# Two transformer blocks on one core: returned expert rows by plain transfers, residual split and identity products later in each engine's order

## The chip, the cores and the metric

The kernel runs on one core of a Trainium2 chip. The metric is the device time of one execution in microseconds (us). A change is judged by the median of several executions of each kernel.

## The reference

Two blocks follow each other, each over 512 tokens of width 1024. Both end with the same kind of step, a mixture of experts (MoE) with two of 32 experts for each token, whose result is added to the residual `h`:

```python
tok_sorted = token_id[order]                 # first block; each token stands twice
hdn = lax.ragged_dot(xt[tok_sorted], w_e_in, group_sizes)
gate_h, up_h = jnp.split(hdn, 2, axis=-1)
ys = lax.ragged_dot(jax.nn.silu(gate_h) * up_h, w_e_out, group_sizes)
ys = ys * gates.reshape(-1)[order][:, None]
y = jnp.zeros_like(xt).at[tok_sorted].add(ys)
...
h = h + y
```

After the first MoE the sum is normalised twice (`rms_norm(h, norm_f_g)`, then the second block's `rmsnorm(h, g_mix)`) and multiplied by `w_in_2`. After the second MoE the sum is normalised with `g_final` and is the output.

## The kernel before, in words

The residual stays in SBUF as `K.h` (`hres` in the trace): four tiles `t` of 128 tokens x 1024. `moe` (from L923) is called twice. It works through 16 pairs of experts `p`; each expert has 64 places for tokens. For a pair, `first_products` (L1467, `gg`) multiplies the gathered tokens by the first weights, `glu` makes `sg` (ACT, then DVE at L1215), `turned` transposes it (`ap`, then `aT`), and `second_products` (L1480, `py`) multiplies by the second weights. The experts' weights stream through a ring of 1 MiB tiles (`rg`), issued on SP's queue in a fixed order (L920).

For pairs 0 to 13 `send` scales the rows and scatters them into a DRAM buffer `yd` by an indirect DMA of POOL's queue (L1264): each token has a row in the first half of `yd` (slot k = 0) and one in the second half (k = 1). After the last scatter `come_back` (L1267) brings `yd` back with eight transfers of 512 KiB on POOL's queue. In the second MoE all eight are accumulating DMAs into `K.h` (L1278). In the first MoE the four of k = 0 are accumulating and the four of k = 1 are plain loads into tiles `yb` (L1276), which take the place of the inputs' tiles `xnh`; `add_back` (L1283) adds them on DVE.

The rows of pairs 14 and 15 never go to DRAM. `gated` (L1240) splits the scaled rows into a high part (ACT, L1252) and a low part (DVE, L1253), both `y`, and makes a 0/1 matrix `C` (DVE, L1246 and L1247) that says which token each row belongs to. The first MoE multiplies `C` by `y` into PSUM (`combine`, L1293) and adds that to `K.h` (L1296).

The second MoE ends the kernel. There class `Sums` builds the final sum in PSUM (`f`): tile 0 of `K.h` by products with the identity in fp32 (`whole`, L1308), tiles 1 to 3 by `split` into a rounded high part (ACT, L1312) and a low part (DVE, L1313), which `halves` multiplies by a rounded identity (L1320). `add` (L1325) puts `C` times `y` on top. Tile 3 gets pair 14 by L1549 and L1551 first. `finish` then squares, normalises and writes the output. There `py_14` and `py_15` are late: their weights are the last of the stream, those of pair 15 in pieces.

What stands around the first MoE's end: `dense2` transposes `K.h` (`n2p`, L1726) into `ah` (ACT, L1727) and `al` (DVE, L1728), loads the first tiles `wr` of `w_in_2` (SP, L124), splits them into `wh` (ACT, L135) and `wl` (DVE, L138) and starts its products (`acc`, L146 to L148). POOL loads the gain row `gf` (L1720) and multiplies it with `K.h` into `fq` (L1739); ACT sums the squares of `fq` (`fk`, L230).

Each engine works its own list in order. The list is made when the program is built, by a scheduler that places an instruction as its inputs are expected; `after(K, x, y)` holds x behind y in the list and adds no wait on the chip. Tiles that lie in the same SBUF space wait for each other by semaphores.

## Time and profile before

| what | value |
|---|---|
| three runs | 1801.83, 1801.61, 1795.31 us; median 1801.61 |
| the profiled execution | 1793.93 us, its span 1792.2 us |
| PE busy | 1667.5 us (93%) |
| DVE, ACT, POOL busy | 796.2, 523.1, 297.7 us |
| DMA | 403.72 MB, mean 225 GB/s |
| end of the first MoE, first tiles of the second block | about 850 to 905 us |
| last stretch of the kernel, from the last scatter | 1701.6 to 1792.2 us |

Times in the trace count from the span's start. "Idle before <-X" in a timeline is idle time of that engine that X ended. A DMA's time runs from its issue to its landing. PEclk is the granted TensorE clock as a share of full speed: 1.00 is 2.4 GHz and 0.50 is 1.2 GHz.

### The profile page before, as it was taken

Reading aid. Unit: us, or ns where it says so; the run is one execution under the profiler, and the core shown is the slowest. Engines: PE = TensorE matmul, PEld = TensorE weight load, DVE = VectorE, ACT = ScalarE, POOL = GpSimd, SP = SyncE. Lnnn points to the kernel's source line nnn. Section 1 sums busy time; section 2 is a strip of 40 time slices with the busy share of each in tenths; the row PEclk is TensorE's granted clock in tenths of the full one; section 3 lists DMA queues with packets and bytes.
Section 4 is the critical chain, followed back from the end, with each engine's and each line's share of the span. In section 5 each row is a group of like instructions: output and inputs, shape, how many; then the busy total and the mean of one; then the engine's idle time right before and its main releaser. Section 6 shows DMA issues by size and latency. Waiting matters only on the chain. (4 is left out here: it accounts for less than half of the span.)

```text
span 1792.2 us, 22864 instructions
## 1 busy us (share of the span) xinstructions
PE 1667.5 (93%) x8960; PEld 1098.2 (61%) x8960; DVE 796.2 (44%) x1843; ACT 523.1 (29%) x898; POOL 297.7 (17%) x325
## 2 busy tenths in 40 slices
PE   6999999999999999999699999899999999999936
PEld 5977877788788754454397976788544433443303
DVE  5688845463346823321554388877411112111003
ACT  3333345662334201101335377534200000000002
POOL 1033211110211000000322267530000000000010
PEclk8999999999999999999899999999999999999978
DMA  4322321234733499999632210217699999999992
GB/s 133 98 73 69 96 81 51 66 112 117 270 98 141 188 420 406 421 418 380 193 95 59 86 45 3 69 48 317 265 419 419 420 419 419 419 421 419 420 326 88
DMA packets 112656, 403.72 MB, mean 225 GB/s; under 512 B 21950, under 2 KB 44478, under 8 KB 75936
## 3 DMA queue, kind: packets, MB, share of 16 engines
q1 hardware_dynamic: 102624, 376.63, 54.5%
q0 software_dynamic: 8880, 25.58, 4.6%
q8 instruction: 72, 1.18, 0.3%
q14 instruction: 40, 0.33, 0.1%
q10 hardware_dynamic: 1040, 0.00, 0.0%
HBM read 382.44 MB, written 27.26 MB: 229 GB/s over the span
## 5 line engine op out<-in xcount | busy, mean ns | idle before, releaser
L1467 PE MATMUL gg<-rg,xT 128*64 128x512 f32 x1536 | 374.3, 597 | 9.3 <-DMA rg<-in_w_expert_gate 4.9
L1467 PEld LDWEIGHTS gg<-rg,xT 128*64 128x64 f32 x1536 | 112.8, 136 | 212.8 <-issue 184.8
L1480 PE MATMUL py<-rg,aT 128*64 128x512 f32 x768 | 196.1, 602 | 16.3 <-DMA rg<-in_w_expert_down 16.3
L135 ACT ACTIVATE wh<-wr 128x1024 fp32r<-128x1024 f32 (+2 forms) x116 | 119.6, 1034 | 249.1 <-PE acc L148 119.2
L138 DVE TENSOR_TENSOR wl<-wr,wh 128x1024 fp32r<-128x1024 f32 (+2 forms) x97 | 118.9, 1227 | 158.2 <-ACT wh L135 157.2
L1480 PEld LDWEIGHTS py<-rg,aT 128*64 128x64 f32 x768 | 57.8, 138 | 134.8 <-issue 103.7
L1264 POOL DMA_INDIRECT yd<-ys,to x28 | 28.0, 998 | 655.5 <-DVE ys L1263 494.9
L146 PE MATMUL acc<-wh,xh 128*128 128x512 f32 (+2 forms) x320 | 122.5, 384 | 8.1 <-DVE xl L260 8.1
L1215 DVE SCALAR_TENSOR_TENSOR sg<-gg,gsl,sg 128x256 f32<-128x256 f32 (+1 forms) x32 | 19.7, 617 | 234.2 <-PE gg L1467 155.1
L148 PE MATMUL acc<-wl,xh 128*128 128x512 f32 (+2 forms) x320 | 122.3, 383 | 0.0
L147 PE MATMUL acc<-wh,xl 128*128 128x512 f32 (+2 forms) x320 | 122.0, 381 | 0.0
L1059 DVE TENSOR_TENSOR xT<-xp,gT 128x512 f32<-128x512 f32 x56 | 38.6, 690 | 152.5 <-PE xp L1056 151.4
L1226 ACT ACTIVATE aT<-ap 128x256 f32<-128x256 f32 (+1 forms) x32 | 15.7, 490 | 282.2 <-PE ap L1223 282.2
L1262 ACT ACTIVATE ys<-py,gsl 128x512 f32<-128x512 f32 x28 | 19.3, 688 | 258.2 <-PE py L1480 152.1
L1263 DVE TENSOR_SCALAR ys<-py,gsl 128x512 f32<-128x512 f32 x28 | 21.0, 751 | 135.0 <-PE py L1480 128.6
L146 PE MATMUL acc<-xh,wh 128*128 128x512 f32 x192 | 77.6, 404 | 0.0
L147 PE MATMUL acc<-xh,wl 128*128 128x512 f32 x192 | 76.7, 400 | 0.0
L148 PE MATMUL acc<-xl,wh 128*128 128x512 f32 x192 | 76.6, 399 | 0.0
L146 PEld LDWEIGHTS acc<-wh,xh 128*128 128x128 f32 x320 | 60.9, 190 | 20.3 <-DVE xl L260 8.3
L147 PEld LDWEIGHTS acc<-wh,xl 128*128 128x128 f32 x320 | 61.0, 191 | 11.7 <-issue 0.7
L148 PEld LDWEIGHTS acc<-wl,xh 128*128 128x128 f32 x320 | 60.6, 190 | 11.6
L138 POOL TENSOR_TENSOR wl<-wr,wh 128x1024 fp32r<-128x1024 f32 x19 | 45.5, 2398 | 124.9 <-DVE wl L138 66.6
(791 smaller groups left out, 3541.1 us busy)
## 6 DMA issues: line engine op xcount, KB each, us to landing
rg<-in_w_expert_in SPq DMA_DIRECT2D x64, 1024.0 KB, 11.3
rg<-in_w_expert_gate SPq DMA_DIRECT2D x64, 1024.0 KB, 20.0
rg<-in_w_expert_up SPq DMA_DIRECT2D x64, 1024.0 KB, 20.4
rg<-in_w_expert_down SPq DMA_DIRECT2D x62, 1024.0 KB, 20.5
wr<-in_w_in SPq DMA_DIRECT2D x84, 512.0 KB, 3.6
rg<-in_w_expert_out SPq DMA_DIRECT2D x32, 1024.0 KB, 12.1
yd<-zeros POOLq DMA_DIRECT2D x2, 4096.0 KB, 21.5
wr<-in_w_out SPq DMA_DIRECT2D x13, 512.0 KB, 3.8
```

The costliest lines, as they stand in the source:

```text
L135: self.high = nc.scalar.activation(wh, raw, AF.Copy)
L138: self.low = low.tensor_tensor(wl, raw, f32(wh), op=ALU.subtract)
L146: nc.tensor.matmul(out, ah, bh, start=first, stop=False)
L147: nc.tensor.matmul(out, al, bh, start=False, stop=False)
L148: return nc.tensor.matmul(out, ah, bl, start=False, stop=last)
L1059: nc.vector.tensor_tensor(xT[:, k2 * 2:k2 * 2 + 2, :], ps, gT[:, kk:kk + 2, None].to_broadcast([128, 2, n]), op=ALU.mult)
L1215: K.gated = nc.vector.scalar_tensor_tensor(sg, ps_u, scale, sg, op0=ALU.mult, op1=ALU.mult)
L1262: nc.scalar.activation(y[:, 0:512], py[0], AF.Copy, scale=gate)
L1263: nc.vector.tensor_scalar(y[:, 512:D], py[1], gate, None, op0=ALU.mult)
L1264: nc.gpsimd.indirect_dma_start(yd, bass.IndirectOffsetOnAxis(ap=rows, axis=0), y, None, bounds_check=ROWS - 1, oob_is_err=False)
L1467: in_turn(nc.tensor.matmul(pss[i][64 * s:64 * s + 64, :], xT[kk // 4][:, kk % 4, c0 + 64 * s:c0 + 64 * s + 64], wt[2 * p + s, nm, kk // 4] ...
L1480: m = nc.tensor.matmul(py[q][64 * s:64 * s + 64, :], aT[:, f, 64 * s:64 * s + 64], wt[2 * p + s, second, f // 2][:, f % 2, q * 512:(q + 1) ...
```

## The change

All eight returned transfers of both MoEs become plain loads. They go into tiles that take the place of `xnh` (k = 0) and `xnl` (k = 1), and DVE adds all eight to `K.h`. In the first MoE the four adds of k = 0 are held behind the low rows of pair 14 and the four of k = 1 behind the last `combine` add. In the second MoE all eight stand behind `K.gated`, the last `sg`. There the block with `whole`, `split` and `halves` moves behind `py_14` and its `gated`: the splits are held behind the last high (ACT) and low (DVE) row parts, and `py_14` now counts in the chain that keeps PE's products in program order (`in_turn`).

```diff
@@ -1231,7 +1231,7 @@
                 return pss[0][:, 0:F], pss[0][:, F:2 * F]
             return pss[0], pss[1]
 
-        behind = [None]
+        behind, hi_of, lo_of = [None], [None], [None]
 
         def in_turn(m):
 
@@ -1251,6 +1251,7 @@
                 yh, yl = y[:, 0, :], y[:, 1, :]
                 hi = nc.scalar.activation(yh, py[q], AF.Copy, scale=gate)
                 lo = nc.vector.scalar_tensor_tensor(yl, py[q], gate, f32(yh), op0=ALU.mult, op1=ALU.subtract)
+                hi_of[0], lo_of[0] = hi, lo
                 if q == 0:
                     K.rows_high, K.rows_low = hi, lo
                 ys.append((yh, yl))
@@ -1266,21 +1267,18 @@
 
         def come_back():
 
-
-            xs = []
+            xs = [[], []]
             for k in range(2):
                 for t in range(NT):
-                    src = yd[k * T + t * 128:k * T + t * 128 + 128, :]
-                    if k and not nlast:
-                        xs.append((xc if t > 1 else xn).tile([128, D], F32, name=f"yb{t}" + sfx, tag=f"xnh{t}", bufs=1))
-                        nc.gpsimd.dma_start(xs[-1], src)
-                    else:
-                        nc.gpsimd.dma_start(K.h[:, t, :], src, accum_op=ALU.add)
+                    xs[k].append((xc if t > 1 else xn).tile([128, D], F32, name=f"yb{k}{t}" + sfx, tag=f"xn{'hl'[k]}{t}",
+                                                            bufs=1))
+                    nc.gpsimd.dma_start(xs[k][t], yd[k * T + t * 128:k * T + t * 128 + 128, :])
             return xs
 
-        def add_back(xs):
+        def add_back(xs, behind):
+
             for t, x in enumerate(xs):
-                after(K, nc.vector.tensor_add(K.h[:, t, :], x, K.h[:, t, :]), K.gated)
+                after(K, nc.vector.tensor_add(K.h[:, t, :], x, K.h[:, t, :]), behind)
 
         def combine(rows, q, part, pss):
 
@@ -1293,7 +1291,7 @@
                     nc.tensor.matmul(pss[t], C[:, t * 128:(t + 1) * 128], y, start=(part + i == 0), stop=(part + i == 2))
                 if part:
                     hs = K.h[:, t, q * 512:(q + 1) * 512]
-                    nc.vector.tensor_add(hs, pss[t], hs)
+                    K.summed = nc.vector.tensor_add(hs, pss[t], hs)
 
 
         class Sums:
@@ -1309,8 +1307,8 @@
                                               stop=False), behind[0])
 
             def split(self, t, hi, lo):
-                nc.scalar.activation(hi, K.h[:, t, :], AF.Copy)
-                nc.vector.tensor_tensor(lo, K.h[:, t, :], f32(hi), op=ALU.subtract)
+                after(K, nc.scalar.activation(hi, K.h[:, t, :], AF.Copy), hi_of[0])
+                after(K, nc.vector.tensor_tensor(lo, K.h[:, t, :], f32(hi), op=ALU.subtract), lo_of[0])
                 self.parts[t] = hi, lo
 
             def halves(self, t, tag, identr):
@@ -1480,7 +1478,7 @@
                 m = nc.tensor.matmul(py[q][64 * s:64 * s + 64, :], aT[:, f, 64 * s:64 * s + 64],
                                      wt[2 * p + s, second, f // 2][:, f % 2, q * 512:(q + 1) * 512],
                                      start=(f == 0), stop=(f == NF - 1))
-                if p not in late:
+                if p not in late[1:]:
                     in_turn(m)
             return py
 
@@ -1522,26 +1520,30 @@
         if not late:
             pss = [[], []]
             rows = [gated(py, *places(NPAIR - 2), None, xt)]
-            add_back(xs)
+            add_back(xs[0], lo_of[0])
             combine(rows, 0, 0, pss[0])
             fetch(NF)
             rows.append(gated(second_products(NPAIR - 1, aT), *places(NPAIR - 1)))
             combine(rows, 0, 1, pss[0])
             for part in range(2):
                 combine(rows, 1, part, pss[1])
+            add_back(xs[1], K.summed)
         for _ in steps:
             pass
         if late:
+            for x in xs:
+                add_back(x, K.gated)
             sums = Sums()
-            sums.whole(0, "c")
             hi, lo = ([ring.place([128, 2, D], F32R) for i in range(2)] for j in range(2))
             identr = wk1.tile([128, 128], F32R, name="identr", tag="sg", bufs=turns)
             nc.scalar.activation(identr, K.ident, AF.Copy)
+            fetch(per - 4 * len(first))
+            py = second_products(late[0], aTs[late[0]])
+            C, ys = gated(py, *places(late[0]))
+            sums.whole(0, "c")
             for t in (1, 2):
                 sums.split(t, hi[t // 2][:, t % 2, :], lo[t // 2][:, t % 2, :])
-            fetch(per - 4 * len(first))
             sums.halves(1, "tp", identr)
-            C, ys = gated(second_products(late[0], aTs[late[0]]), *places(late[0]))
             t = NT - 1
             for q in range(2):
                 ps = bank(f"c{q}{t}l", "g")
```

The schedule follows from this. Names carry their tile's number here: `y014` is half 0 of pair 14, `y114` half 1, `yb12` token tile 2 of the returned rows (slot k = 1 where no slot is named; in the new kernel `yb00` to `yb03` are k = 0 and `yb10` to `yb13` are k = 1, a further digit 1 or 2 being the MoE), `c00` to `c13` the sums of `combine`.

DVE at the end of the first MoE, from the last `sg`, before:

```order
L1215 SCALAR_TENSOR_TENSOR sg15_6912<-gg0_15_6890,gsl1_5092,sg15_6912 128x256
L1283 TENSOR_TENSOR hres_60<-yb01_6882,hres_60 128x1024
L1283 TENSOR_TENSOR hres_60<-yb11_6884,hres_60 128x1024
L1283 TENSOR_TENSOR hres_60<-yb21_6886,hres_60 128x1024
L1253 SCALAR_TENSOR_TENSOR y014_6933<-py0_14_6915,gsl1_5092,y014_6933 128x512
L1283 TENSOR_TENSOR hres_60<-yb31_6888,hres_60 128x1024
L1253 SCALAR_TENSOR_TENSOR y114_6936<-py1_14_6916,gsl1_5092,y114_6936 128x512
```

and now:

```order
L1215 SCALAR_TENSOR_TENSOR sg15_6916<-gg0_15_6894,gsl1_5092,sg15_6916 128x256
L1253 SCALAR_TENSOR_TENSOR y014_6937<-py0_14_6919,gsl1_5092,y014_6937 128x512
L1253 SCALAR_TENSOR_TENSOR y114_6940<-py1_14_6920,gsl1_5092,y114_6940 128x512
L1281 TENSOR_TENSOR hres_60<-yb001_6878,hres_60 128x1024
L1281 TENSOR_TENSOR hres_60<-yb011_6880,hres_60 128x1024
L1281 TENSOR_TENSOR hres_60<-yb021_6882,hres_60 128x1024
L1281 TENSOR_TENSOR hres_60<-yb031_6884,hres_60 128x1024
L1253 SCALAR_TENSOR_TENSOR y015_6972<-py0_15_6959,gsl1_5092,y015_6972 128x512
```

The two low parts of pair 14 stood behind three and four adds of returned rows and now stand ahead of all of them.

DVE a little later, around the last `combine` adds and the first work of the second block, before:

```order
L1296 TENSOR_TENSOR hres_60<-c11_6989,hres_60 128x512
L1296 TENSOR_TENSOR hres_60<-c12_6992,hres_60 128x512
L1296 TENSOR_TENSOR hres_60<-c13_6995,hres_60 128x512
L1744 ISA fj0_7135,fsa_7131<-hres_60 128x1024
L1744 ISA fsa_7131 128x1
L1759 MEMSET hv_7046 128x16
L1767 MEMSET am_7045 128x256
L1728 SCALAR_TENSOR_TENSOR al_7044<-n2p0_7069,vecs_77,ah_7043 128x512
```

and now:

```order
L1294 TENSOR_TENSOR hres_60<-c12_6996,hres_60 128x512
L1294 TENSOR_TENSOR hres_60<-c13_6999,hres_60 128x512
L1281 TENSOR_TENSOR hres_60<-yb101_6886,hres_60 128x1024
L1281 TENSOR_TENSOR hres_60<-yb111_6888,hres_60 128x1024
L1281 TENSOR_TENSOR hres_60<-yb121_6890,hres_60 128x1024
L1281 TENSOR_TENSOR hres_60<-yb131_6892,hres_60 128x1024
L1927 MEMSET skT3_7294 128x16
L1932 MEMSET vmp0_7300 64x128
L1746 ISA fj0_7143,fsa_7139<-hres_60 128x1024
```

Four adds of returned rows now stand between the last `combine` add and the second block. `wl0` and `wl1` (L138), which stood among the `combine` adds (rows further up), now follow `al` and the second sum of squares, `fj2`.

DVE at the end of the second MoE, before:

```order
L1313 TENSOR_TENSOR rg2195_13476<-hres_60,rg2193_13474 128x1024
L1313 TENSOR_TENSOR rg2196_13477<-hres_60,rg2194_13475 128x1024
L1215 SCALAR_TENSOR_TENSOR sg15_13460<-gg1_15_13420,gsl2_11080,sg15_13460 128x512
L1246 TENSOR_SCALAR C15_13563<-sfr2_11083,sid_5007 128x512
L1247 SCALAR_TENSOR_TENSOR C15_13563<-sfr2_11083,sid_5007,C15_13563 128x512
L1253 SCALAR_TENSOR_TENSOR y014_13511<-py0_14_13490,gsl2_11080,y014_13511 128x512
L1253 SCALAR_TENSOR_TENSOR y114_13514<-py1_14_13491,gsl2_11080,y114_13514 128x512
L1551 TENSOR_TENSOR hres_60<-c03l_13517,hres_60 128x512
L1551 TENSOR_TENSOR hres_60<-c13l_13521,hres_60 128x512
```

and now:

```order
L1215 SCALAR_TENSOR_TENSOR sg15_13476<-gg1_15_13436,gsl2_11088,sg15_13476 128x512
L1281 TENSOR_TENSOR hres_60<-yb002_13413,hres_60 128x1024
L1281 TENSOR_TENSOR hres_60<-yb012_13415,hres_60 128x1024
L1281 TENSOR_TENSOR hres_60<-yb022_13417,hres_60 128x1024
L1281 TENSOR_TENSOR hres_60<-yb032_13419,hres_60 128x1024
L1281 TENSOR_TENSOR hres_60<-yb102_13421,hres_60 128x1024
L1281 TENSOR_TENSOR hres_60<-yb112_13423,hres_60 128x1024
L1281 TENSOR_TENSOR hres_60<-yb122_13425,hres_60 128x1024
L1281 TENSOR_TENSOR hres_60<-yb132_13427,hres_60 128x1024
L1246 TENSOR_SCALAR C15_13587<-sfr2_11091,sid_5007 128x512
L1247 SCALAR_TENSOR_TENSOR C15_13587<-sfr2_11091,sid_5007,C15_13587 128x512
L1253 SCALAR_TENSOR_TENSOR y014_13521<-py0_14_13500,gsl2_11088,y014_13521 128x512
```

Before, two residual splits stood ahead of the last `sg`. Now `sg` comes first, eight adds follow, and `C` and the low parts of pair 14 stand behind the eighth.

PE at the same place, before:

```order
L1480 MATMUL py0_14_13490<-rg2185_13325,aT14_13442 64x512
L1223 MATMUL ap15_13463<-ident_78,sg15_13460 128x128 x4
L1308 MATMUL f00_13470<-hres_60,ident_78 128x512
L1308 MATMUL f01_13471<-hres_60,ident_78 128x512
L1320 MATMUL f10_13484<-rg2193_13474,identr_13478 128x512
L1320 MATMUL f10_13484<-rg2195_13476,identr_13478 128x512
L1320 MATMUL f11_13485<-rg2193_13474,identr_13478 128x512
L1320 MATMUL f11_13485<-rg2195_13476,identr_13478 128x512
L1480 MATMUL py0_14_13490<-rg2186_13327,aT14_13442 64x512
```

and now:

```order
L1478 MATMUL py1_14_13501<-rg2187_13337,aT14_13458 64x512
L1478 MATMUL py1_14_13501<-rg2188_13383,aT14_13458 64x512
L1478 MATMUL py1_14_13501<-rg2187_13337,aT14_13458 64x512
L1478 MATMUL py1_14_13501<-rg2188_13383,aT14_13458 64x512
L1306 MATMUL f00_13527<-hres_60,ident_78 128x512
L1306 MATMUL f01_13528<-hres_60,ident_78 128x512
L1318 MATMUL f10_13535<-rg2193_13494,identr_13498 128x512
L1318 MATMUL f11_13536<-rg2193_13494,identr_13498 128x512
L1551 MATMUL c03l_13541<-y014_13521,C14_13518 128x512 x2
L1551 MATMUL c13l_13545<-y114_13524,C14_13518 128x512 x2
```

The products with the identity stood between the transposes `ap15` and the rest of `py_14` and now follow all of `py_14`.

## Rows read from the trace of the kernel before

**Rows 1.** Chain of the last 153 us: start us, us, what

```profile
1701.55 7.72 DMA yd<-ys,to
...
1729.60 18.37 DMA hres<-yd
```

**Rows 2.** Timeline of PE, kernel's end: start us, us, engine, line

```profile
1716.36 3.65 PE L1467 MATMUL gg<-rg,xT 128*64 128x512 f32 x14 [2.47 <-DMA rg<-in_w_expert_up]
...
1751.02 1.13 PE L1223 MATMUL ap<-ident,sg 128*128 128x128 f32 x4 [28.54 <-DVE sg L1215]
...
1763.98 0.50 PE L1549 MATMUL c03l<-y,C 128*128 128x512 f32 x1
...
1768.96 6.22 PE L1480 MATMUL py<-rg,aT 128*64 128x512 f32 x26
```

**Rows 3.** Timeline of DVE, same stretch

```profile
1750.22 0.74 DVE L1215 SCALAR_TENSOR_TENSOR sg<-gg,gsl,sg 128x512 f32<-128x512 f32 x1
...
1751.39 0.75 DVE L1247 SCALAR_TENSOR_TENSOR C<-sfr,sid,C 128x512 fp32r<-128x512 uint16 x1
1763.12 0.75 DVE L1253 SCALAR_TENSOR_TENSOR y<-py,gsl,y 128x512 fp32r<-128x512 f32 x1 [10.98 <-ACT y L1252]
```

**Rows 4.** Timeline of POOL, same stretch: issues of the second four accumulating transfers

```profile
1719.57 0.86 POOL L1278 DMA_DIRECT2D hres<-yd  x1 [6.32 <-DMA hres<-yd]
...
1734.57 0.85 POOL L1278 DMA_DIRECT2D hres<-yd  x1 [4.11 <-DMA hres<-yd]
```

**Rows 5.** Windows: us, busy PE PEld DVE ACT POOL, PEclk, DMA share, GB/s

```profile
1710.00:1760.00 50.00, 17.32 (x58) 6.73 (x60) 4.25 (x5) 4.41 (x6) 6.68 (x8) 0.69 0.88 267
1724.00:1726.00 2.00, 0.00 (x0) 0.00 (x0) 0.00 (x0) 0.00 (x0) 0.86 (x1) 0.98 1.03 303
1755.00:1757.00 2.00, 2.00 (x7) 1.02 (x5) 0.00 (x0) 0.00 (x0) 0.00 (x0) 0.59 0.08 27
```

**Rows 6.** DMA queues, 1720 to 1730: packets, MB, share of 16 engines

```profile
q0 software_dynamic: 294, 1.07, 53.7%
q1 hardware_dynamic: 291, 2.03, 50.5%
```

**Rows 7.** DMA queue of POOL, 857 to 864 (accumulating transfers alone)

```profile
q0 software_dynamic: 396, 1.43, 104.8%
```

**Rows 8.** DMA packets and queue, 867 to 871 (plain loads alone)

```profile
DMA packets 458, 1.67 MB, mean 418 GB/s; under 512 B 50, under 2 KB 50, under 8 KB 458
...
q0 software_dynamic: 458, 1.67, 102.1%
```

**Rows 9.** Timeline of PE, end of the first MoE

```profile
871.95 3.35 PE L1293 MATMUL c<-y,C 128*128 128x512 f32 x7 [12.35 <-DVE y L1253]
...
902.87 0.28 PE L146 MATMUL acc<-ah,wh 128*128 128x264 f32 x1
```

**Rows 10.** Timeline of DVE, same stretch

```profile
867.51 3.72 DVE L1283 TENSOR_TENSOR hres<-yb,hres 128x1024 f32<-128x1024 f32 x3 [10.98 <-DMA yb<-yd]
...
885.24 1.88 DVE L1296 TENSOR_TENSOR hres<-c,hres 128x512 f32<-128x512 f32 x3
```

**Rows 11.** Timeline of ACT, same stretch

```profile
858.97 0.69 ACT L1252 ACTIVATE y<-py,gsl 128x512 fp32r<-128x512 f32 x1 [1.03 <-PE py L1480]
...
889.56 1.07 ACT L230 ACTIVATE fk<-fq 128x1024 bf16<-128x1024 f32 x1
```

**Rows 12.** Timeline of POOL, same stretch

```profile
859.66 0.53 POOL L1720 DMA_DIRECT2D gf<-in_norm_f_g  x1 [0.83 <-PE ap L1223]
...
886.00 11.38 POOL L1739 TENSOR_TENSOR fq<-hres,gf 128x1024 f32<-128x1024 f32 x4 [3.89 <-DVE hres L1296]
```

**Rows 13.** Timeline of SP, same stretch

```profile
873.06 12.66 SPq L124 DMA_DIRECT2D wr<-in_w_in  x4
```

**Rows 14.** DMA issues of the whole span: KB each, median us to landing

```profile
sgc<-in_sgu_b POOLq DMA_DIRECT2D x1, 512.0 KB, 5.2
gf<-in_norm_f_g POOLq DMA_DIRECT2D x1, 512.0 KB, 12.9
```

## Prediction

> **What bounds the kernel now.** I read the chain of waits first. At its end the last scatter lands at 1701.55 + 7.72 = 1709.27, and the chain then runs through the returned rows until 1729.60 + 18.37 = 1747.97 [rows 1]. The timelines show what that holds up. PE has finished the first products of pair 15 at 1716.36 + 3.65 = 1720.0 and stands idle for 28.54 us until DVE's `sg` lets the transposes go at 1751.02 [rows 2]. That `sg` took 0.74 us and had its inputs since 1720, but two residual splits stand ahead of it in DVE's list and wait for accumulated rows, so it ran at 1750.22 [rows 3]. The rest of the kernel hangs on it: `c03l` at 1763.98, `py_15` at 1768.96 [rows 2].
>
> The rows come late because accumulating is slow. POOL issues its second four transfers as the first four land, 1719.57 to 1734.57: three steps of 5.0 us [rows 4]. Alone, accumulating transfers moved 1.43 MB in 7 us, 2.57 us for 512 KiB (0.524 MB) [rows 7]; plain loads moved 1.67 MB in 4 us, 1.26 us for the same [rows 8]. Beside the weights both queues passed as many packets, 294 and 291, for 1.07 and 2.03 MB [rows 6]: 512 KiB of rows to each 1 MiB tile of weights. That checks: 1.05 MB of weights at 418 GB/s is 2.51 us, and 2.57 + 2.51 = 5.08, near the 5.0 seen.
>
> The same pattern stands at the end of the first MoE. PE waits 12.35 us, until 871.95, for the low half of pair 14's rows [rows 9]. DVE had waited 10.98 us for returned rows and then made three adds, 867.51 to 871.23, ahead of it [rows 10], while ACT's second high half started at 858.97 [rows 11].
>
> **The second MoE.** The first four rows lose the accumulation, and the second four also their wait for the first. One row beside one weight tile should cost 1.26 + 2.51 = 3.77 us instead of 5.0. The first lands 1.3 us earlier than the 1719.3 of now, at 1718; the eighth 7 x 3.77 = 26.4 later, at 1744.4. A second estimate: between 1710 and 1760 the core moved 267 GB/s x 50 us = 13.35 MB [rows 5], which at 418 GB/s takes 31.9 us, so all is in by 1741.9. I take 1743. The bounds are 1724 (rows served ahead of weights, eight times 1.26 from about 1714) and 1751 (DMA no faster than now).
>
> `sg` no longer waits, so `ap15` follows `gg` at about 1721. `py_14` needs four weight tiles: the last of `gg` let PE go at 1716.36, and 4 x 3.77 later is 1731.4. Of its 32 rows in the trace 22 stand behind the fourth tile; 26 take 6.22 us at full clock [rows 2], so 22 take 5.3, or 10.5 at half: done by 1742. The identity products of tile 0 fit behind them. Both are covered by the wait for the eighth row; without that cover they would be the bound.
>
> DVE adds each row as it lands, 1.23 us (three in 3.72 [rows 10]) inside a step of 3.77. Seven adds are covered; the eighth ends at 1744.3. `C` stood off the path before and now stands behind the eighth add: from the end of `sg` (1750.96) to 1752.14 it took 1.2 [rows 3], so 1745.5. The low half `y014` takes 0.75 [rows 3]: 1746.2. Before, `c03l` followed that row by 0.1, and 4.98 us later `py_15` began [rows 2]. Now two products with tile 1's low part stand in that stretch and wait for its split, a DVE operation over twice the elements of `y` behind `y114`: I add 1.7. So `py_15` begins at 1746.3 + 5.0 + 1.7 = 1753.0 at full clock.
>
> The clock costs some of it. PE last ran at 1722.5 and was granted 0.98 of full speed over 1724 to 1726: it fell to the lower level just before 1726. After work resumed at 1751.02 the mean over 1755 to 1757 was still 0.59, so it rose near 1756.6, 5.6 us later [rows 5]. PE will stand idle from about 1740 to 1746, so it starts `c03l` at 1.2 GHz. Half speed for 5.6 us loses 2.8; part falls into the wait for the split, so I add 2.0. `py_15` then begins at 1755 instead of 1768.96: **-14 us**. Behind it the lists are the same but for one product's place. The bounds are -22 (rows at 1724; `py_15` then follows `py_14` and the late weights, at 1747) and -6 (row at 1751).
>
> The rate of 418 GB/s [rows 8] matters here. The Trainium skill, "DMA: Bandwidth & Descriptors", Specifications, gives about 358 GB/s as what HBM delivers to a core. By that the 13.35 MB would take 37.3 us, the last row would land at 1747.3 and this part would bring about 10 instead of 14; the row shows the higher rate, so the measurement decides.
>
> **The first MoE.** The low halves of pair 14 no longer stand behind adds, so `combine` starts where PE's idle time began, at 871.95 - 12.35 = 859.6. From 871.95 to the last `combine` add (885.24 + 1.88 = 887.12) now takes 15.2 us; a split `wl` leaves that stretch (1.2) and it runs at full clock from its start (1.5): 859.6 + 12.5 = 872.1. The four adds of k = 0 run while PE works on `py_15` and cost nothing there. The four adds of k = 1 come behind: 4 x 1.23 = 4.9, so the residual is complete at 877.0, 10.1 us earlier.
>
> Not all of it is kept, since two transfers get new waits, whose values I read from the built program. The tiles of `gf` and of the first `wr` lie where returned rows lie now. `gf` waits for the second of the last four adds (874.6; it was issued at 859.66 [rows 12]) and `wr` for the fourth (877.0; it was 873.06 [rows 13]). Queued behind `gf` on POOL are the four `fq`, and behind `wr` on SP the later loads. A lone 512 KB transfer of POOL's queue landed in 5.2 us [rows 14]: `gf` at 879.8. The first `fq` takes 11.38 / 4 = 2.85 [rows 12]: 882.6. ACT's list has `fk` (1.07, and 0.2 to read its sum [rows 11]) ahead of the first `wh` (about the same): 885.0. DVE's `wl` takes 1.2: 886.2. Then 48 products of 512 columns at 0.24 (6.22 / 26 [rows 2]) are 11.5, and PE, nearly idle since 872, starts them at the lower clock (2.0 as above): 899.7, where the 264-column products began at 902.87 [rows 9]. **-3 us**. The bounds are -10 (all of the residual's lead kept) and +5: `gf` took 12.9 us in the queue of now [rows 14], which moves it to 887.5 and the 264-column products to 907.4.
>
> No row shows a POOL transfer issued while DVE adds two SBUF tiles, as `gf` will be. The Trainium skill, "SBUF — State Buffer", SBUF: two separate sides, says that descriptors of POOL's transfers cannot be written while DVE holds the port pair it shares with POOL. If these adds held it, `gf` would go out at 877.0 and this part would bring about 1 instead of 3.
>
> **The sum.** -14 - 3 = -17 us. The profiled execution took 1793.93, its span 1792.2 and 1.7 outside it, so it would take 1777. The median of the runs is 7.7 above the profiled execution; -17 against 1801.61 gives **1784**, my forecast.
>
> **The rivals.** *The second block starts later* (0.13). The new waits of `gf` and `wr` cost the upper bound, +5, and the end keeps its -14: 1801.6 - 9 = 1792.6. For it: ACT's list has `fk` ahead of `wh`. Against: the 12.9 us was spent behind eight other transfers.
>
> *Rows ahead of weights* (0.13). POOL's queue gets more than its turn: -22 - 3 = -25, 1776.6. Against it: the equal packets [rows 6].
>
> *The DMA gets no faster* (0.10). Only DVE's order helps: -6 - 3 = -9, 1792.6. For it: the bytes are the same. Against: rows 7 and 8.
>
> *Slower: DVE's eight adds hold pair 14* (0.03). `C` and the low halves wait for the last row whatever it takes. If plain rows beside weights moved at 204 GB/s (1.43 MB in 7 us [rows 7]), the 13.35 MB would end at 1775.4 and `py_15` begin near 1787.4: +18.4 - 3 = +15, 1817. It decides against the change once the last row lands after 1760 (17 us later than 1743 uses up the 17), a mean of 267 GB/s from 1710 on. Rows 8 speak against it.
>
> **Chances and range.** The forecast has 0.61, with its own range 1776 to 1791. A measurement here tells about 0.5%, 9 us, from no change: 1792.6 or less is faster. That holds for the forecast, for rows ahead, and half of the first and third: 0.86. Within 0.5%: 0.11. Slower: 0.03. The range takes in the first three rivals and the distance between the profiled execution and the median: 1768 to 1794.
>
> **What would show it.** Right: `sg` right behind `gg` near 1720, the last add of a returned row near 1743, `py_15` starting 14 us earlier, `combine` near 860, eight loads some 1.3 us apart in the first MoE, `gf` issued near 875. Wrong: returned rows still 5 us apart beside the weights, PE idle again behind DVE's `C`, or `acc` of the second block starting later than before.

## The result and the profile after

| | before | changed |
|---|---|---|
| median of 4 runs each | 1799.64 us (1795.31 to 1801.83) | 1774.47 us (1770.39 to 1777.42) |
| ratio, 95% interval | | 0.9862 [0.9829, 0.9894] |
| profiled execution, span | 1793.93, 1792.2 us | 1777.42, 1775.7 us |

The forecast was 1784 with a range of 1768 to 1794, and faster with 0.86: it was faster by 1.4%. The medians lie 25 us apart, the profiled executions only 16.5. Half of that difference stands ahead of everything the change touches: the second half of `gg_15` in the first MoE starts 4.4 us later in the changed kernel's profile. A stretch of the first block shows one source of it. The windows (columns as in [rows 5]) are of before, then of the change:

```profile
100.00:130.00 30.00, 28.85 (x139) 21.25 (x138) 27.00 (x72) 11.66 (x22) 8.09 (x5) 1.00 0.21 65
```

```profile
100.00:130.00 30.00, 28.89 (x114) 21.14 (x113) 23.17 (x59) 10.09 (x20) 5.36 (x4) 0.72 0.13 37
```

The same stretch of the program had a mean clock of 1.00 in one execution, with 139 products, and 0.72 in the other, with 114. In the 14 profiled executions behind this study that half of `gg_15` starts anywhere from 850.3 to 858.9 us, whatever the kernel. So places are compared from a row of their own: the second half of `gg_15` in the first MoE, POOL's first issue of a returned row in the second, and the end of PE's last product. In before:

```profile
851.84 3.65 PE L1467 MATMUL gg<-rg,xT 128*64 128x512 f32 x16
```

```profile
1709.57 3.68 POOL L1278 DMA_DIRECT2D hres<-yd  x4 [7.05 <-DMA yd<-ys,to]
```

```profile
1781.06 1.08 PE L1325 MATMUL f<-y,C 128*128 128x512 f32 x4
```

and in the changed kernel, first PE at the end of the first MoE, which answers to [rows 9]:

```profile
856.23 3.65 PE L1465 MATMUL gg<-rg,xT 128*64 128x512 f32 x16
...
863.51 2.10 PE L1291 MATMUL c<-y,C 128*128 128x512 f32 x8
...
888.93 1.22 PE L146 MATMUL acc<-ah,wh 128*128 128x512 f32 x2 [3.27 <-ACT wh L135]
...
903.62 0.28 PE L146 MATMUL acc<-ah,wh 128*128 128x264 f32 x1
```

From `gg_15` to the 264-column products it was 902.87 - 851.84 = 51.0 us and is 47.4. `combine` starts at 863.51 without the wait of 12.35 us. DVE there, which answers to [rows 10]:

```profile
864.75 4.62 DVE L1281 TENSOR_TENSOR hres<-yb,hres 128x1024 f32<-128x1024 f32 x4
...
874.63 1.89 DVE L1294 TENSOR_TENSOR hres<-c,hres 128x512 f32<-128x512 f32 x3 [0.64 <-PE c L1291]
876.44 4.62 DVE L1281 TENSOR_TENSOR hres<-yb,hres 128x1024 f32<-128x1024 f32 x4
...
884.87 2.96 DVE L1746 CUSTOM_DVE_ANT_0 fj<-hres 128x1024 bf16<-128x1024 f32 x1
...
888.91 5.55 DVE L138 TENSOR_TENSOR wl<-wr,wh 128x1024 fp32r<-128x1024 f32 x2 [1.07 <-ACT wh L135]
```

The eight adds take 4.62 us for four; the residual is complete at 881.06. Two later rows are slow: the second `fj` took 2.96 us, and the two `wl`, 5.55 together, took 2.23 and 3.40. PE waited only for the first `wl`. POOL, which answers to [rows 12]:

```profile
879.34 0.53 POOL L1722 DMA_DIRECT2D gf<-in_norm_f_g  x1 [17.32 <-DVE hres L1281]
...
884.40 12.33 POOL L1741 TENSOR_TENSOR fq<-hres,gf 128x1024 f32<-128x1024 f32 x4 [3.98 <-DMA gf<-in_norm_f_g]
```

The end of the kernel, PE (answers to [rows 2]):

```profile
1720.98 0.75 PE L1223 MATMUL ap<-ident,sg 128*128 128x128 f32 x4 [0.91 <-DVE sg L1215]
...
1731.52 6.78 PE L1478 MATMUL py<-rg,aT 128*64 128x512 f32 x22 [2.69 <-DMA rg<-in_w_expert_down]
...
1746.21 0.79 PE L1551 MATMUL c03l<-y,C 128*128 128x512 f32 x1 [3.53 <-DVE y L1253]
...
1753.96 7.09 PE L1478 MATMUL py<-rg,aT 128*64 128x512 f32 x32
...
1764.79 1.08 PE L1323 MATMUL f<-y,C 128*128 128x512 f32 x4
```

`ap15` waits 0.91 us instead of 28.54, `py_15` starts at 1753.96 instead of 1768.96, and one wait of 3.53 us for a low half is left at `c03l`. DVE (answers to [rows 3]):

```profile
1720.17 0.75 DVE L1215 SCALAR_TENSOR_TENSOR sg<-gg,gsl,sg 128x512 f32<-128x512 f32 x1 [18.67 <-PE gg L1465]
...
1727.99 1.23 DVE L1281 TENSOR_TENSOR hres<-yb,hres 128x1024 f32<-128x1024 f32 x1 [4.07 <-DMA yb<-yd]
1731.67 1.22 DVE L1281 TENSOR_TENSOR hres<-yb,hres 128x1024 f32<-128x1024 f32 x1 [2.46 <-DMA yb<-yd]
1735.55 1.23 DVE L1281 TENSOR_TENSOR hres<-yb,hres 128x1024 f32<-128x1024 f32 x1 [2.66 <-DMA yb<-yd]
...
1741.13 1.23 DVE L1281 TENSOR_TENSOR hres<-yb,hres 128x1024 f32<-128x1024 f32 x1 [0.55 <-DMA yb<-yd]
1743.08 1.23 DVE L1281 TENSOR_TENSOR hres<-yb,hres 128x1024 f32<-128x1024 f32 x1 [0.73 <-DMA yb<-yd]
...
1745.41 1.40 DVE L1253 SCALAR_TENSOR_TENSOR y<-py,gsl,y 128x512 fp32r<-128x512 f32 x2
```

`sg` runs at 1720.17. From the second on each add starts as its row lands. The third to the sixth are 3.7 to 3.9 us apart instead of 5.0 [rows 4], the last two only 1.8 and 2.0; behind the eighth come `C` and both low halves. POOL's first row went out at

```profile
1710.62 4.31 POOL L1275 DMA_DIRECT2D yb<-yd  x8 [7.40 <-DMA yd<-ys,to]
```

so from there to the end of the last product (1764.79 + 1.08) it is 55.25 us, where before had 1782.14 - 1709.57 = 72.57. DMA queues from 1720 to 1730, which answer to [rows 6]:

```profile
DMA packets 808, 4.14 MB, mean 414 GB/s; under 512 B 89, under 2 KB 89, under 8 KB 494
...
q1 hardware_dynamic: 403, 2.67, 64.5%
q0 software_dynamic: 404, 1.45, 36.6%
```

Both queues still pass as many packets, 403 and 404, but now 404 carry 1.45 MB of rows where 294 carried 1.07.

### The profile page after: what moved, and what is told of

The parts are those of the page before. It is cut to its first block, busy times and chain, and to the rows that moved or that the text cites. A ratio compares the mean times of both kernels' runs of the same rounds, so it can differ in the third digit from the quotient of the medians.

```text
span 1775.7 us, 22892 instructions
## 1 busy us (share of the span) xinstructions
PE 1675.8 (94%) x8958; PEld 1103.8 (62%) x8960; DVE 813.6 (46%) x1855; ACT 522.5 (29%) x898; POOL 293.2 (17%) x325
## 5 line engine op out<-in xcount | busy, mean ns | idle before, releaser
L138 DVE TENSOR_TENSOR wl<-wr,wh 128x1024 fp32r<-128x1024 f32 (+2 forms) x97 | 121.8, 1258 | 161.8 <-ACT wh L135 160.8
L138 POOL TENSOR_TENSOR wl<-wr,wh 128x1024 fp32r<-128x1024 f32 x19 | 45.5, 2395 | 127.7 <-DVE wl L138 67.3
## 6 DMA issues: line engine op xcount, KB each, us to landing
rg<-in_w_expert_in SPq DMA_DIRECT2D x64, 1024.0 KB, 11.5
```

Of the source, the lines that this page charges most:

```text
L138: self.low = low.tensor_tensor(wl, raw, f32(wh), op=ALU.subtract)
```

## The experiments

The table puts all runs together. A is from the second half of `gg_15` (the expectations call it the first; it is the row at 856.23) to the first 264-column product, A+ from the same row at 856.23 to POOL's first issue of a returned row in the second MoE, B from that issue to the end of the last product, all from the profiled execution of each. "Before" ran beside each group; its medians were 1795.12 (runs 1 to 4), 1794.5 (5 to 8), 1799.49 (9 to 11) and 1795.08 us (12).

| kernel | median us | ratio, 95% | A | A+ | B |
|---|---|---|---|---|---|
| before | 1799.64 | | 51.0 | 857.7 | 72.6 |
| change | 1774.47 | 0.9862 [0.9829, 0.9894] | 47.4 | 854.4 | 55.3 |
| 1 second MoE alone | 1778.95 | 0.9897 [0.9865, 0.9928] | 51.4 | 858.5 | 56.4 |
| 2 first MoE alone | 1789.67 | 0.9969 [0.9950, 0.9989] | 47.1 | 853.8 | 71.6 |
| 3 order alone | 1780.75 | 0.9916 [0.9888, 0.9945] | 51.6 | 858.2 | 59.2 |
| 4 products as before | 1776.14 | 0.9898 [0.9857, 0.9938] | 51.2 | 857.9 | 55.3 |
| 5 gf, wr early | 1777.70 | 0.9905 [0.9886, 0.9925] | 48.8 | 858.8 | 54.6 |
| 6 lows first | 1772.10 | 0.9880 [0.9858, 0.9902] | 47.3 | 854.5 | 51.8 |
| 7 two queues | 1771.42 | 0.9857 [0.9828, 0.9887] | 47.1 | 854.2 | 50.8 |
| 8 both | 1771.60 | 0.9868 [0.9850, 0.9887] | 47.4 | 854.5 | 54.1 |
| 9 change again | 1774.95 | 0.9870 [0.9849, 0.9890] | 47.4 | 853.8 | 55.8 |
| 10 5, 6, fq on DVE | 1775.50 | 0.9872 [0.9854, 0.9890] | 41.7 | 856.9 | 50.7 |
| 11 7, fq on DVE | 1774.71 | 0.9867 [0.9848, 0.9886] | 46.6 | 856.9 | 50.7 |
| 12 4 and 7 | 1771.23 | 0.9862 [0.9839, 0.9885] | 47.0 | 854.0 | 49.9 |

The theory going in: the two places act on their own, and in the second MoE faster rows and DVE's order share the gain as the prediction's steps have it. The rival: the order is nearly all of it.

**Runs 1 and 2: one place at a time.** Run 1 leaves the first MoE as it was, run 2 the second.

```diff
 # run 1, come_back
-xs[k].append(...); nc.gpsimd.dma_start(xs[k][t], src)
+if late or k: xs[k].append(...); nc.gpsimd.dma_start(xs[k][t], src)
+else: nc.gpsimd.dma_start(K.h[:, t, :], src, accum_op=ALU.add)
 # run 2, come_back; the block "if late:" and split as before
+if late: nc.gpsimd.dma_start(K.h[:, t, :], src, accum_op=ALU.add)
```

> The change at the second MoE alone, the first MoE as before. The trace of the change has py_15 at 1753.96 instead of 1768.96, 15.0 us earlier. Theory (the two places act independently, the second MoE carries most): 14 to 17 us below the kernel before, about 1784, ratio 0.990 to 0.992. Rival (the measured 25 us holds a share of the first MoE that the two profiled executions hide): the second MoE alone stays at 15 and the first alone, in the next run, shows 8 or more.

> The change at the first MoE alone, the second as before. Theory: 3 to 4 us below the kernel before (the 264-column products start 3.65 us earlier relative to the same point ahead of the place), about 1796, ratio 0.998. Rival (the residual's lead of 10 us is kept): 8 to 10 us below, ratio 0.995. Rival (the new waits of gf and wr cost more than the lead): 0 to 5 us above.

Run 1 is 1.0% below before, run 2 0.3%. In run 1 the first place stands as in before (A 51.4) and B as in the change; in run 2 it is the other way round. The two add up and neither touches the other, and both theories hold in the main: the medians differ from before by 16.2 us (14 to 17 expected) and by 5.5 (3 to 4 expected, 3.9 by A+). With the kernel's first MoE as before A+ is 857.7 to 858.5, with the change's own 853.8 to 854.5: -3.9 us. B is 72.6 and 71.6 without the change and 55.3, 55.8 and 56.4 with it: -16.3. Run 5 below, whose second MoE is the change's too, has 54.6; so B of the same work spreads over 1.8 us, and a smaller difference between two single traces says nothing. Together the places bring 20, which the intervals of the change's two comparisons (0.9862 and 0.9870) hold at their upper ends, 0.989. The other 5 of the 25 us may be spread of the runs, since before's ran from 1792 to 1802 through the whole study; that is not shown.

**Runs 3 and 4: order or transfers.** Run 3 has the change's order at the second MoE with accumulating transfers, so no adds on DVE; the first MoE as before. Run 4 has plain loads and adds, with products and splits at their old place.

```diff
 # run 3: before, and in the block "if late:"
 sums = Sums()
-sums.whole(0, "c")
...
-for t in (1, 2): sums.split(...)
 fetch(per - 4 * len(first))
+py = second_products(late[0], aTs[late[0]])
+C, ys = gated(py, *places(late[0]))
+sums.whole(0, "c")
+for t in (1, 2): sums.split(...)
 # run 4: before with eight plain loads, and in the block "if late:"
+add_back(xs)
 sums = Sums()
 sums.whole(0, "c")
```

> At the second MoE the order of the change with the accumulating transfers of before: no adds on DVE, sg ahead of the splits, identity products behind py_14. The first MoE as before. By the steps of the prediction (transfers set the end, order alone brings 6): py_15 starts near 1763, 6 us below the kernel before. Rival (the order was the whole delay): the last accumulated rows land where they did, 1747.97 for tile 2 and 1751.3 for tile 3, but py_14, C and the low halves no longer wait for them and tile 3 is needed only behind py_15; then a split, four products and the sums follow 1748, py_15 starts at 1753 to 1755, 13 to 15 us below, and the plain transfers bring nothing of their own.

> At the second MoE plain loads and eight adds behind the last sg, but the residual's identity products and splits keep their place ahead of and between py_14's products. The first MoE as before. Theory (each product of py_14 behind an identity product waits for the row tile of that product): py_14 ends at 1746 or later, its high and low halves near 1748, py_15 at 1756 to 1758, 11 to 13 us below the kernel before. Rival (the place of the identity products does not matter once sg is free): the same as the second MoE alone, 15 below.

Run 3, POOL, DVE and PE:

```profile
1708.41 3.68 POOL L1279 DMA_DIRECT2D hres<-yd  x4 [7.20 <-DMA yd<-ys,to]
...
1734.56 0.85 POOL L1279 DMA_DIRECT2D hres<-yd  x1 [4.20 <-DMA rg<-in_w_expert_down]
```

```profile
1718.17 0.75 DVE L1215 SCALAR_TENSOR_TENSOR sg<-gg,gsl,sg 128x512 f32<-128x512 f32 x1 [18.67 <-PE gg L1468]
...
1750.77 0.69 DVE L1553 TENSOR_TENSOR hres<-c03l,hres 128x512 f32<-128x512 f32 x1 [1.01 <-DMA hres<-yd]
```

```profile
1746.05 0.63 PE L1551 MATMUL c03l<-y,C 128*128 128x512 f32 x2
...
1755.65 7.09 PE L1481 MATMUL py<-rg,aT 128*64 128x512 f32 x32
```

The rows come as slowly as in before: the last accumulating transfer went out 26.2 us behind the first (25.0 in before) and its tile was added to at 1750.77. Still `py_15` starts 47.2 us behind the first issue, where before had 1768.96 - 1709.57 = 59.4 and the change has 43.3. With `sg` free, `py_14`, `C` and the low halves are done ahead of the late rows, `c03l` runs at 1746.05, and only tile 3 needs the last one. B is 59.2: of the 16.3 us the order alone brings 12.9, plain rows and their adds together 3.4 on top of it. The rival came near with its 13 to 15, the theory's 6 did not; that plain rows bring nothing of their own does not hold by the trace (the medians of runs 1 and 3, 1.8 us apart, cannot tell). No run has plain rows with `sg` still behind the splits, so what the rows bring without the order is not measured.

Run 4 equals the change: B 55.3 in both. Its PE

```profile
1734.18 3.75 PE L1310 MATMUL f<-hres,ident 128*128 128x512 f32 x4 [8.81 <-DVE hres L1285]
...
1751.65 7.09 PE L1482 MATMUL py<-rg,aT 128*64 128x512 f32 x32
```

waits 8.81 us for the fifth add and lets `py_14` end late, as expected, but then no identity products are left behind it. `py_15` starts 43.4 us behind the first issue, as in the change. So with plain rows the new place of the identity products is worth nothing once `sg` stands ahead of them.

**Run 5: gf and wr early.** The first MoE's tiles of k = 0 and k = 1 change places, and the last adds go from the high tiles to the low ones.

```diff
-tag=f"xn{'hl'[k]}{t}"
+tag=f"xn{'hl'[k] if late else 'lh'[k]}{t}"
-for t, x in enumerate(xs):
+for t, x in sorted(enumerate(xs), key=lambda j: j[0], reverse=back):
```

> The change, but in the first MoE the returned tiles of k = 0 and k = 1 change places and the last four adds run from the high tiles to the low ones. gf then waits for an add of k = 0 and the first wr for the second of the last four adds. Theory (the two transfers' new waits hold back what the residual's lead could bring): gf goes out near 867 instead of 879 and wr 2.3 us earlier, fk no longer stands late ahead of wh, and from the first half of gg_15 to the 264-column products it takes 44.5 to 45.5 us instead of 47.4, so 2 to 3 us below the changed kernel. Rival (DVE, busy from the first add to the end of the last, and the slow wl beside fq set the start): 0 to 1 us below it.

```profile
863.76 0.53 POOL L1722 DMA_DIRECT2D gf<-in_norm_f_g  x1 [5.61 <-PE py L1478]
...
877.42 13.15 POOL L1741 TENSOR_TENSOR fq<-hres,gf 128x1024 f32<-128x1024 f32 x4 [8.98 <-DVE lb L1807]
```

```profile
877.20 1.22 DVE L1746 CUSTOM_DVE_ANT_0 fj<-hres 128x1024 bf16<-128x1024 f32 x1
...
878.46 3.26 DVE L1746 CUSTOM_DVE_ANT_0 fj<-hres 128x1024 bf16<-128x1024 f32 x1
...
881.65 3.35 DVE L138 TENSOR_TENSOR wl<-wr,wh 128x1024 fp32r<-128x1024 f32 x1
...
888.24 2.71 DVE L1730 SCALAR_TENSOR_TENSOR al<-n2p,vecs,ah 128x512 fp32r<-128x512 f32 x4
```

Counted from `gg_15` (852.34 here), `gf` goes out 11.7 us and `fq` starts 3.1 us earlier than in the change, and the second block comes later: A 48.8, A+ 858.8, all of the first place's gain lost. The first `fj`, begun just ahead of POOL's first `fq`, took 1.22 us; `fj` and `wl` behind it took 3.26 and 3.35, while four `al`, which read PSUM, kept 0.68 each. Both theory and rival expected a gain. With `fq` on POOL the new waits are no cost on balance: they also keep `fq` out of DVE's way.

**Runs 6 to 8: what is left in the second MoE.** Run 6 puts `C` and the low halves of pair 14 ahead of the last four adds; run 7 issues every second row on ACT's queue; run 8 does both.

```diff
 # run 6
-for x in xs: add_back(x, K.gated)
+add_back(xs[0], K.gated)
 C, ys = gated(py, *places(late[0]))
+add_back(xs[1], lo_of[0])
 # run 7
-nc.gpsimd.dma_start(xs[k][t], ...)
+(nc.scalar if late and t % 2 else nc.gpsimd).dma_start(xs[k][t], ...)
```

> The change, but in the second MoE C and the low halves of pair 14 stand behind the first four adds and ahead of the last four. Theory (the eight adds ahead of C take back what the faster rows bring): the wait of 3.53 us at c03l goes, PE uses it for products with pair 14 and the first of py_15, and the last product ends 43.9 to 46 us behind the one that lets sg go instead of 47 or more; 3 to 4 us below the changed kernel, ratio to before about 0.986. Rival (the eighth row is the bound): splits and sums of tiles 1 to 3 wait for it anyway and the time stays within 1 us of the changed kernel.

> The change, but in the second MoE the rows of tiles 1 and 3 are issued on ACT's DMA queue, those of 0 and 2 on POOL's. Theory (queues share by packets, so two queues of rows get two shares beside one of weights): one pair of rows beside one weight tile, the eighth row lands near 1728 instead of 1743, C and the low halves follow py_14 at 1740, the wait at c03l goes: 3 to 5 us below the changed kernel; the last weights still land near 1747. Rival (the rows on ACT hold ACT until the scatter has landed and delay pair 14's transposed copy): py_14 later, 0 to 3 us above it. Rival (rows and weights share by bytes): landings as before, no difference.

> Both edits of the two runs before this one together. Theory: with the rows early the sums no longer wait for them at all, and what is left is PE's own work behind the last weights; 5 to 8 us below the changed kernel. Rival: the two edits remove the same wait once, so 3 to 5 us below, as either alone.

Run 6, PE:

```profile
1734.15 0.73 PE L1551 MATMUL c03l<-y,C 128*128 128x512 f32 x2
1734.81 1.07 PE L1478 MATMUL py<-rg,aT 128*64 128x512 f32 x2
```

Its `c03l` follows `py_14` at once and PE fills the wait with the first of `py_15`: B 51.8, 3.4 us below the change. So the eight adds ahead of `C` did take back about half of what the faster rows brought: from run 3, where `C` also stands ahead of the late rows, to run 6 it is 59.2 - 51.8 = 7.4 us, and the change keeps 3.9 of them (3.4 by the mean of its three traces). Run 7, SP and DVE, and last what SP waited for from 1700 to 1725 (us in total, times, longest us):

```profile
1695.25 12.79 SPq L920 DMA_DIRECT2D rg<-in_w_expert_up  x4
1720.57 15.33 SPq L920 DMA_DIRECT2D rg<-in_w_expert_down  x10
```

```profile
1725.99 9.26 DVE L1281 TENSOR_TENSOR hres<-yb,hres 128x1024 f32<-128x1024 f32 x8
```

```profile
SPq L920 <- DMA yb<-yd: 14.6, 2, 12.5
```

All eight adds run back to back; the last ends 22.2 us behind POOL's first issue (33.7 in the change). B is 50.8, 4.5 less. The rows gain that by more than two shares of three would give them: SP issues no weights between 1708 and 1720.57, and waits for a returned row through those 12.5 us. In the built program SP's and ACT's transfers share their completion counters, so SP's next weight transfer waits for a row of ACT's to land (read from the program; no run gave them counters apart). Run 8 gains nothing on either, B 54.1: its last four adds now stand behind low halves that come later than the rows. By their ratios, 0.9857 to 0.9880, runs 6 to 8 are not to be told from the change.

**Runs 9 to 11: the change again, and fq on DVE.**

```diff
 # runs 10 (with 5 and 6) and 11 (with 7)
-nc.gpsimd.tensor_tensor(q[:, t, :], K.h[:, t, :], gf, op=ALU.mult)
+after(K, nc.vector.tensor_tensor(q[:, t, :], K.h[:, t, :], gf, op=ALU.mult), low)
```

> The changed kernel once more, beside the kernel before on the same chip. If the two places are all there is (3.7 us and 15 to 16 us by the trace), it is 19 to 21 us below the kernel before, ratio 0.988 to 0.9895. If the 25 us of the first comparison (ratio 0.9862) hold, there is a further gain that the two places do not show.

> The edits of the runs on the early gf and wr and on the low halves first, and in addition fq is multiplied by DVE behind its second wl instead of by POOL. Theory for the first MoE (fq on POOL slows DVE's fj and wl, 2.7 to 3.4 us each where 1.2 was usual; this and not gf's wait holds the second block): fj and wl take about 1.2 us again and from the first half of gg_15 to the 264-column products it takes 43 to 45 us instead of 48.8 (early gf and wr) or 47.4 (the change). Rival (DVE's own four products cost as much as they free): 47 or more. At the second MoE the gain of 3.4 us is repeated: altogether 5 to 8 us below the changed kernel by the theory, 3 to 4 by the rival.

> fq on DVE behind its second wl, with gf and wr where the change has them, and the rows of the second MoE on two queues. Theory: first MoE 45 to 46.5 us for the same stretch (wl at 1.2 us, but wr still late); second MoE 4 us less than the change, as in the run with two queues: 5 to 6 us below the changed kernel. Rival (DVE's own products cost what they free): 47 or more, and 3 to 5 us below.

Run 9 repeats the result: 24.5 us, more than the 19 to 21 of the two places, with an interval that still takes in 0.989. A further gain is neither shown nor ruled out. Run 10's DVE

```profile
876.92 1.22 DVE L1747 CUSTOM_DVE_ANT_0 fj<-hres 128x1024 bf16<-128x1024 f32 x1
...
878.27 1.22 DVE L138 TENSOR_TENSOR wl<-wr,wh 128x1024 fp32r<-128x1024 f32 x1
```

has `fj` and `wl` back at 1.22 us with the same early `gf` and `wr` as run 5, and A falls to 41.7. That shows POOL's `fq` as the cause of the slow rows. But A+ is 856.9: the sums of squares now come late, PE waits for the norm they feed,

```profile
899.71 2.40 PE L1760 MATMUL n2al<-n2dg,onef 128*128 128x128 f32 x8 [2.55 <-DVE n2dg L1759]
```

and the stretch from 900 to 920 had a mean clock of 0.76 (1.00 in run 9). In run 11, where `gf` and `wr` stay late, A gains only 0.8, although its `wl` take 1.23 us: `wh` waits for `wr`.

```profile
883.41 1.06 ACT L135 ACTIVATE wh<-wr 128x1024 fp32r<-128x1024 f32 x1 [1.99 <-DMA wr<-in_w_in]
```

So with `fq` off POOL the new waits do cost, 46.6 - 41.7 = 4.9 us of A. Run 11's A+ loses 2.6 as well, with a mean clock of 0.91 from 900 to 920. Neither run can be told from the changed kernel beside it, where 5 to 8 and 5 to 6 us less were expected.

**Run 12: two queues and products as before.** The change with the edit of run 7 and with the block of run 4.

```diff
 # run 12, beside run 7's line; split and in_turn as before
 sums = Sums()
+sums.whole(0, "c")
...
-fetch(per - 4 * len(first))
-py = second_products(late[0], aTs[late[0]])
-C, ys = gated(py, *places(late[0]))
-sums.whole(0, "c")
 for t in (1, 2): sums.split(...)
+fetch(per - 4 * len(first))
 sums.halves(1, "tp", identr)
+C, ys = gated(second_products(late[0], aTs[late[0]]), *places(late[0]))
```

> The change's first MoE, plain loads and eight adds, the rows of the second MoE on two queues, and there the identity products and splits in the kernel before's place, ahead of and between py_14's products. Theory (with the rows in by 20 us behind their first issue, the identity products fall into PE's waits for py_14's weights): from the first row's issue to the end of the last product 46 to 48 us instead of 50.8 with two queues alone and 55.5 in the changed kernel; 7 to 9 us below the changed kernel, ratio to before 0.982 to 0.984. Rival (PE waits for a row or a split between py_14's products as long as it saves): 50 to 52 us, ratio 0.985 to 0.987.

B is 49.9, the shortest, but only 0.9 below run 7 where the theory has 3 to 5, and that is within the spread of B: the rival's 50 to 52 is nearer. Its median, 1771.23, and ratio, 0.9862, are not to be told from the change's. No version here beats the changed kernel by more than can be measured.

## Why the prediction was right, and where it was not

**First MoE, -3 (measured -3.6 at the 264-column products, -3.9 by A+).** With 4.4 us added for the later start, each step stands in the trace within 0.6 us: `combine` 864.0 (863.51), its last add 876.5 (874.63 + 1.89), residual complete 881.4 (881.06), `gf` out 879.0 (879.34), landed 884.2 (`fq` starts at 884.40), 264-column products 904.1 (903.62). Two terms were off by 1.0 and cancel, which is luck: the `wl` that PE waited for was put at 1.2 and took 2.23, and the products behind it, put at 11.5 + 2.0, took 12.5 (903.62 less the end of that `wl` at 891.14). And the reason, "two transfers get new waits", is only half of it. Run 5 took `gf`'s wait away and brought `wr` 2.3 us forward, and lost 4.4 us by A+; run 10 shows that the multiplication on POOL stands in DVE's way. The waits hold the start too, as run 11 shows; only with both gone (run 10) does A keep nearly all of the residual's lead of 10 us, 51.0 - 41.7 = 9.3, and there A+ gives most of it back. The sum put nothing for the multiplication on POOL, though the kernel before has the same slow rows beside its `fq` [rows 12], 2.42 us for the `fj` at 887.03 and 2.92 for the next:

```profile
892.20 2.92 DVE L1744 CUSTOM_DVE_ANT_0 fj<-hres 128x1024 bf16<-128x1024 f32 x1
```

The Trainium skill, "SBUF — State Buffer", SBUF: two separate sides, states such an exclusion: an operation of DVE with two SBUF inputs and one of POOL that reads SBUF lock each other out for the whole instruction. The traces agree: beside `fq`, `fj` and `wl` took 2.2 to 3.4 us instead of 1.2, and `al`, which reads PSUM, kept its 0.68. The prediction drew on another sentence of that section (descriptors of POOL's transfers held up by DVE); no run shows that: `gf` went out between the adds, at 879.34, and had landed 5.1 us later, as alone [rows 14].

**Second MoE, -14 (measured -15.0 at `py_15`, -16.1 counted from POOL's first row, B -16.3 over the runs).** The steps: eighth add ending at 1744.3 (1743.08 + 1.23 = 1744.3), `py_14` done by 1742 (1738.3), the first low half at 1746.2 (1745.41 + 0.75), `py_15` 1755 (1753.96). POOL's first row went out 1.05 us later than before, so counted from there the eighth add and the low half came 1 us sooner than the sum and `py_15` 2 us. An even pitch of 3.77 is not what the rows had: 5.3 us ahead of the third, then 3.7 to 3.9, at the end 1.8 and 2.0; that the eighth landed where the sum has it is in part luck. The clock fell as expected: windows of PE,

```profile
1744.00:1746.00 2.00, 0.00 (x0) 0.00 (x0) 1.97 (x4) 0.00 (x0) 0.00 (x0) 0.66 0.20 77
1746.00:1748.00 2.00, 1.65 (x3) 0.79 (x4) 2.00 (x4) 0.00 (x0) 0.00 (x0) 0.50 0.09 36
1752.00:1754.00 2.00, 2.00 (x11) 1.36 (x9) 0.62 (x1) 0.00 (x0) 0.00 (x0) 1.00 0.00 0
```

The clock was at 1.2 GHz behind an idle stretch of PE, and at full speed again from 1752 on. From the second `c03l` to `py_15` it took 7.75 us, where the sum had 5.0 + 1.7 + 2.0 = 8.7 from `c03l` on: one of its two additions, for the split and for the clock, was too much. Behind `py_15` "the lists are the same but for one product's place"; that place was worth 1.3 us, since before its products were cut in two [rows 2] and from their start to the end of the last product it was 13.2 us (1782.14 - 1768.96), now 11.9. The rate from 1720 to 1730 was 414 GB/s (4.14 MB in 10 us). The Trainium skill, "DMA: Bandwidth & Descriptors", Specifications, gives about 358 GB/s for a core; this trace passes that again, as [rows 8] did, and no sum goes by it.

**What the prediction had wrong is the order's share,** "Only DVE's order helps: -6" in the third rival. That is a price for the kernel as built, with `C` and the low halves behind the eighth add, in case the rows come no faster; no run has that case. But it is not what the order can bring: run 3, without adds, has nothing there that waits for all rows, and brought 12.9 with rows as slow as before. So the -14 was right for the kernel as built, but not as 6 for the order and the other 8 for the transfers: the order alone is worth four fifths, the faster rows 3.4 on top of it, and about as much again is lost by the place of `C` (run 6).

**From the profile to the median.** -17 was to be taken from a median 7.7 us above the profiled execution: 1784. The sum was short by 3, and the median of three was a sample from 1792 to 1802. Measured side by side it is -25 and -24.5, of which the places account for 20; where the other 5 come from stays open.

## What to carry to other kernels

Ask first which instruction of an engine's list waits for a late transfer although it does not need it; moving that one earned 12.9 us here, and faster transfers 3.4 on top of it. When rows are added by an engine instead of by the DMA, the adds take a place in that engine's list, and what is put behind the last of them waits for the last row. Compare places from a row of their own: over the profiled executions one row ahead of both places started up to 8.6 us apart, twice what the smaller place was worth. Taking one wait away may only uncover the next: in the first MoE `gf`'s wait and the multiplication on POOL had both to go before the block started much earlier, and even then a later step gave most of it back.

## What the hardware showed

A multiplication of POOL over 128x1024 floats slowed DVE's operations with two SBUF inputs from 1.2 us to between 2.2 and 3.4, and not those that read PSUM (0.68 us). Rows on a second queue went ahead of the weights by holding up their issue (SP waited 12.5 us for one of them in run 7), which no share of bandwidth would have told.
